# Six context FFN blocks inside the latents' output product, and the next layer's conditioning spread over the FFN

## The chip, the cores and the metric

The kernel runs on one core of a Trainium2 chip. The metric is device time in microseconds (us). The engines are TensorE (PE; its weight loads PEld are listed apart), VectorE (DVE), ScalarE (ACT), GpSimd (POOL) and SyncE (SP), which issues most transfers. Each engine works through its own list in order, so an instruction that waits holds back all that stands behind it on its engine.

## What is computed

Two layers work on 256 latent tokens and 256 context tokens of width 1024. Each layer has three head groups (A, B, C), one output projection, a post-layer-norm, an FFN and a second post-layer-norm; the shifts, scales and gates come from a conditioning product with `w_ada`. The part that matters here is the end of layer 0 and the way into its FFN:

```python
p = jnp.split(_modulate(x, sh1, sc1) @ w_in[li], IN_OFFSETS, axis=-1)     # latents; pc: context
yd, ydc = _diff_attn(p[7], p[8], p[9], pc[7], pc[8], pc[9], ...)          # head group C
mix = jnp.concatenate([ya, yb, yd], axis=-1) @ w_out[li]
x = _post_ln(ALPHA * x + g1 * mix, ln1_g[li], ln1_b[li])
x = _post_ln(ALPHA * x + g2 * ffn(_modulate(x, sh2, sc2)), ln2_g[li], ln2_b[li])
# the same for ctx with yac, ybc, ydc in layer 0
def _swiglu(h, w_gu, w_down):
    g, u = jnp.split(h @ w_gu, 2, axis=-1)
    return (jax.nn.silu(g) * u) @ w_down
```

Context tokens read only context tokens. The FFN of layer 0 has 2816 hidden columns, 22 blocks of 128; layer 1 has eight experts instead.

## The kernel before

**Tiles.** The 512 tokens are four tiles of 128: 0 and 1 are the context, 2 and 3 the latents. Activations are kept transposed in `HI` and `LO` (a rounded part and the rest), 256 columns for each half. Each product is done three times by `mm3`: HI by the weights' rounded part (L273), LO by it (L274), HI by the weights' rest (L276). A weight is loaded to `raw`, rounded by ACT to `whi` (L259), and its rest `wlo` (L260) is made by DVE or POOL. `raw` has 4 buffers, `whi` and `wlo` 3 each.

**How the order comes about.** Generators yield estimated costs; `weave` takes next from the one with the least cost over its weight, `"?name"` waits until some generator has yielded `"+name"`. `PLAN[0]` names the order of the attention tasks: A0 to A3 and C0 to C3 are head groups and tiles, and `/` starts a second stream. What each engine then has in its list is what the rows of order below show.

**The end of layer 0.** `tail0` runs `out_ab` (the output product of groups A and B, PSUM name `op`, 256 columns wide), then `out_c` (that of group C, `op` 512 wide) for each of the pairs (0, 1) and (2, 3). In `attn_C` a tile's scores are `SC`, its weights `P`, transposed to `PT`, its heads `yC`; after an RMS norm (`rstd_of`, tile `nw`, a chain of ten short DVE instructions; L942 applies it) `yC` is transposed (`py`, L952) and split into HI and LO. `CH` names the tiles whose group C is done in two halves. Behind `out_c` comes the post-layer-norm of the tile (`otmp`, L245 statistics, `rstd_of`, L479, L480), then a second layer norm (`layernorm`: statistics, `rstd_of`, `nmr` on DVE, `lnx` on ACT), and `make_hT`, which transposes both tiles of a half on PE (L433, `hT`, 16 of them), modulates them on ACT and leaves the FFN's HI and LO.

**Between.** `ada_group(L1, 0)` follows: sixteen loads of 512 KB of `w_ada` and 64 matmuls (`ada`, L316, two records each in the trace) for layer 1.

**FFN.** `gate_up` makes a block of 128 hidden columns: 2 (gate, up) x 8 (k) x 3 products, 48 matmuls (`gu`), weights of 1 MB in four loads of 256 KB; silu, product, and the split into `ah` and `al`. The first `M0` = 3 blocks are done for the context and then for the latents, 256 columns wide; the other eight of the first half for both, 512 wide. Then the first half of the down product (`dn`), then blocks 11 to 21 and its second half.

Of the kernel before, what the change touches and what calls it, by code (L numbers as in the profile page):

```python
# [12 lines left out]
F = mybir.dt.float32  # L13
# [18 lines left out]
FT = 22  # L32
NE = 8
BIG = 1.0e30
M0 = 3
LOP = 0, 1
KP = 1, 0
XC = 0, 4
LNB, LRB = 3, 7
RO = 2  # L40
CH = (3,), ()
KG = 4
XB, START, MRB, MSB = 1, 1, (5, 1, 5), 4

# [7 lines left out]
TOKT, TRA, ADA = "S", "tp", "S"  # L52
T1, T2, T3, T4, T5, T6, T7, T8, T9 = "y", "tp", "mm", "S", "S", "S", "mm", "tp", "tp"
OPT = 'mm'
HTD = 1
TL0 = CTX, LAT
DNP = 1
DN = ((0, CTX), (1, CTX), (0, LAT), (1, LAT))
# [7 lines left out]

# [48 lines left out]
def kernel(ctx: ExitStack, tc: tile.TileContext, I, out: bass.AP):  # L115
# [21 lines left out]
    def p_(tag, name):  # L137
        return ps.tile([128, 512], F, name=name, tag=tag, bufs=NBUF[tag])
# [79 lines left out]
        return (I["ctx"] if t in CTX else I["x"])[0, (t % 2) * 128:(t % 2 + 1) * 128]  # L218


    def rstd_of(v, n, scale=1.0):


        a = sm.tile([128, 3, 8], F, name="nw", tag="nw", bufs=6)
        ve, y, t = (a[:, i, :n] for i in range(3))
        iv = sm.tile([128, 2, 8], I32, name="nwi", tag="nwi", bufs=6)
# [12 lines left out]
        V.tensor_scalar(y, y, 1.0 / f, None, op0=OP.mult)  # L239
        return y  # L240
# [178 lines left out]

    def layernorm(pool, xs, t):  # L420
        mu, rs = ln_stats(xs[t])
        n = pool.tile([128, D], F, name="lnx", tag="lnx", bufs=LNB if pool is lp else 4)
        nm = sm.tile([128, 1], F, name="nmr", tag="nmr")
        V.scalar_tensor_tensor(nm, mu, -1.0, rs, op0=OP.mult, op1=OP.mult)
        S.activation(n, xs[t], AF.Identity, scale=rs, bias=nm)
        return n
# [76 lines left out]
        return ap.rearrange("p (h d) -> p h d", h=h)  # L503


    def mixers(L, full_ctx, fill, tail):
# [326 lines left out]
        def ssd_finish(t, y):  # L833
            z = zcol(t, 0, 384)
            th = sp.tile([128, 384], F, name="zth", tag="yB", bufs=3)
            S.activation(r4(th, 3), z, AF.Tanh, scale=0.5)
            V.scalar_tensor_tensor(r4(th, 3), r4(th, 3), 1.0, z, op0=OP.add, op1=OP.mult)
            V.scalar_tensor_tensor(y, y, 0.5, th, op0=OP.mult, op1=OP.mult)
            ss = sm.tile([128, 1], F, name="ss", tag="ss")
            S.activation(th, y, AF.Square, accum_out=ss)  # L840
            rs = rstd_of(ss, 1, 1.0 / 384)
            V.scalar_tensor_tensor(y, y, rs, L.snw, op0=OP.mult, op1=OP.mult)
            put_y(t, y, 3, 3)

# [61 lines left out]
        def attn_C(t):  # L906
# [4 lines left out]
            for h in range(4):  # L911
# [25 lines left out]
                if h % 2 and t in CH[li] or h == 3:  # L937
                    a = h - 1 if t in CH[li] else 0
                    n_ = h + 1 - a
                    rs = rstd_of(ss[:, a:h + 1], n_, 1.0 / 64)  # L940
# [101 lines left out]
        weave((1.0, chain(blend(dense_gen(), chain(*fill), nfill, SKIP[li]), tail)),  # L1042
              *((wa[i] if type(wa) is tuple else wa, attention(n)) for i, n in enumerate(streams)), (ws, task("S")))

    def out_consts(L, tiles, pp):

# [80 lines left out]
            post_ln(xs[t], *L.ln1, LN1[t - 2] if L.li else None)  # L1127
            yield t

    def ffn(L, pp, done):  # L1130
        li = L.li
        xs = L.xs
        W = I["ffn_w_gu"][0].rearrange("(k p) (a n) -> p k a n", p=128, a=2)
# [4 lines left out]
        act = {}  # L1138

        def gate_up(f, s):  # L1140
            wk = kpieces(lambda k0: [((slice(None), slice(None), a), W[:, k0:k0 + 4, a, f * 128:(f + 1) * 128])
                                     for a in range(2)], [128, 4, 2, 128])
            o = slice(s.start * 256, s.stop * 256)
            pg = [p_("S", "gu"), p_("mm", "gu")]
            for a in range(2):
                for k0 in range(0, KC, KG):
                    mm3(pg[a][:, o], [(wk(k)[0][:, a], wk(k)[1][:, a], HI[:, s, k], LO[:, s, k], True)
                                      for k in range(k0, k0 + KG)], k0 == 0, k0 + KG == KC)
            sl = L.pp.tile([128, 512], F, name="silu", tag="otmp", bufs=OT)
            S.activation(sl[:, o], pg[0][:, o], AF.Silu)  # L1150
            V.tensor_tensor(sl[:, o], sl[:, o], pg[1][:, o], op=OP.mult)
            if f not in act:
                act[f] = (pp.tile([128, 512], FR, name="ah", tag="ah", bufs=11),
                          pp.tile([128, 512], FR, name="al", tag="al", bufs=11))
            ah, al = act[f]
            S.activation(ah[:, o], sl[:, o], AF.Copy)
            V.tensor_tensor(al[:, o], sl[:, o], ah[:, o].bitcast(F), op=OP.subtract)

        for half in range(2):
            f0 = 11 * half  # L1160
            n0 = 0 if half else M0

            for s in range(2):
                for f in range(f0, f0 + n0):
                    gate_up(f, slice(s, s + 1))
            for f in range(f0 + n0, f0 + 11):
                gate_up(f, slice(0, 2))
            for c, tiles in ((0, (0, 1, 2, 3)), (1, (0, 1, 2, 3))) if half == 0 else DN:
                cs_ = slice(c * 512, (c + 1) * 512)
                tags = ("S", "mm") if len(tiles) == 2 else FDN[c]  # L1170
# [2 lines left out]
                for n in (2, 2, 2, 2, 2, 1):  # L1173
                    src = Wd[f0 * 128:(f0 + n) * 128, cs_].rearrange("(f p) n -> p f n", p=128)
                    wh, wl = split(load_w([(None, src)], [128, n, 512]), [128, n, 512],
                                   G if len(tiles) == 2 and DNP else V)
                    for t in tiles:
                        ts_ = slice(t * 128, (t + 1) * 128)
                        mm3(pd[t], [(*(x[:, ts_] for x in act[f0 + i]), wh[:, i], wl[:, i], False) for i in range(n)],
                            f0 == 11 * half, f0 + n == 11 * half + 11)  # L1180
                    f0 += n
                for t in tiles:
# [539 lines left out]
    def tail0():  # L1722
        yield "?S"
        pp = L0.pp = L0.tp = post.enter_context(tc.tile_pool(name="post0", bufs=1))
        out_consts(L0, range(NT), pp)
        ns = {}
        for tiles in TL0:
            yield from out_ab(L0, tiles, pp)
            for v in out_c(L0, tiles, pp):
                if type(v) is int:  # L1730
                    ns[v] = layernorm(pp, L0.xs, v)
                    if v == 1:
                        if HTD == 1:
                            yield "?att"
                        if HTD < 2:
                            make_hT(pp, L0.mod2, ns, 0)
                    if v == 3:
                        if HTD == 2:
                            make_hT(pp, L0.mod2, ns, 0)
                        make_hT(pp, L0.mod2, ns, 1)  # L1740
# [73 lines left out]
```

## Time and profile before

| | before |
|---|---|
| time, median of 3 runs | 1819.24 us (1816.98 to 1824.41) |
| the profiled execution | 1821.04 us |
| its span in the trace | 1819.2 us |
| PE busy | 1663.7 us, 91% of the span |
| DVE busy | 1154.5 us, 63% |
| ACT busy | 874.4 us, 48% |
| POOL busy | 321.9 us, 18% |
| DMA | 436.09 MB, mean 240 GB/s |

The profiled execution's time is 1.84 us above its span, the part outside the first and the last instruction; its own time is 1.8 us over the median. Busy shares are averages over a program of stages; in the stretch that the change touches (300 to 575 us) every engine has its own limits.

### The profile page before, as it was taken

Reading aid. Unit: us, or ns where it says so; the run is one execution under the profiler, and the core shown is the slowest. Engines: PE = TensorE matmul, PEld = TensorE weight load, DVE = VectorE, ACT = ScalarE, POOL = GpSimd, SP = SyncE. Lnnn points to the kernel's source line nnn. Section 1 sums busy time; section 2 is a strip of 40 time slices with the busy share of each in tenths; the row PEclk is TensorE's granted clock in tenths of the full one; section 3 lists DMA queues with packets and bytes.
Section 4 is the critical chain, followed back from the end, with each engine's and each line's share of the span. In section 5 each row is a group of like instructions: output and inputs, shape, how many; then the busy total and the mean of one; then the engine's idle time right before and its main releaser. Section 6 shows DMA issues by size and latency. Waiting matters only on the chain.

```text
span 1819.2 us, 26372 instructions
## 1 busy us (share of the span) xinstructions
PE 1663.7 (91%) x9454; PEld 1244.2 (68%) x9454; DVE 1154.5 (63%) x2224; ACT 874.4 (48%) x1447; POOL 321.9 (18%) x254
## 2 busy tenths in 40 slices
PE   5898989887999999987999984899999999999995
PEld 2677657674988888876786672487686685784782
DVE  4673668658632343288587756288785586982895
ACT  3433545543622132335444652376673574772770
POOL 1221013334420022474232141000000000000000
PEclk8999998878999999999899996899999999999998
DMA  9327454328633233345676227999999999999995
GB/s 306 86 67 236 127 149 123 107 66 269 188 93 96 89 101 96 110 165 167 209 223 207 65 82 300 395 406 409 408 406 376 399 406 409 406 408 387 408 407 229
DMA packets 248153, 436.09 MB, mean 240 GB/s; under 512 B 15025, under 2 KB 166329, under 8 KB 248017
## 3 DMA queue, kind: packets, MB, share of 16 engines
q1 hardware_dynamic: 246096, 429.55, 66.2%
q0 software_dynamic: 1920, 4.81, 1.0%
q8 instruction: 76, 1.25, 0.3%
q14 instruction: 61, 0.49, 0.1%
HBM read 431.08 MB, written 3.23 MB: 239 GB/s over the span
## 4 chain that ended last, share of the span: by engine, by line
PE 77%; DMA 8%; DVE 7%; issue 2%; ACT 2%; POOL 0%; SPq 0%; ACTq 0%; DVEq 0%; POOLq 0%
PE mg L1369 6%; PE mu L1369 6%; PE mdn L1369 5%; PE gu L273 5%; PE gu L274 5%; PE gu L276 4%; DMA raw<-in_w_ada 4%; PE mu L1358 3%; PE mg L1358 3%; PE mdn L1358 3%; PE tok L276 2%; DMA mraw<-in_exp_w_gu 2%; PE ada L316 2%; PE tok L273 2%; PE SC L919 2%; PE tok L274 2%
## 5 line engine op out<-in xcount | busy, mean ns | idle before, releaser
L1349 DVE TENSOR_TENSOR mwl<-mraw,mwh 128x1024 fp32r<-128x1024 f32 (+1 forms) x350 | 389.4, 1160 | 37.2 <-ACT mwh L1348 20.2
L1348 ACT ACTIVATE mwh<-mraw 128x1024 fp32r<-128x1024 f32 (+1 forms) x350 | 337.8, 1013 | 61.4 <-PE mg L1369 22.9
L260 POOL TENSOR_TENSOR wlo<-raw,whi 128x1024 fp32r<-128x1024 f32 (+2 forms) x93 | 224.1, 2416 | 482.2 <-ACT whi L259 435.1
L259 ACT ACTIVATE whi<-raw 128x1024 fp32r<-128x1024 f32 (+2 forms) x168 | 168.2, 1004 | 237.3 <-PE dn L274 71.9
L260 DVE TENSOR_TENSOR wlo<-raw,whi 128x1024 fp32r<-128x1024 f32 (+2 forms) x75 | 90.5, 1206 | 144.1 <-ACT whi L259 142.8
L273 PE MATMUL gu<-HI,whi 128*128 128x512 f32 (+1 forms) x400 | 144.2, 369 | 2.3 <-ACT whi L259 2.3
L274 PE MATMUL gu<-LO,whi 128*128 128x512 f32 (+1 forms) x400 | 144.9, 369 | 0.0
L273 PE MATMUL tok<-whi,HI 128*128 128x256 f32 (+2 forms) x400 | 108.7, 301 | 5.4 <-ACT xin L550 4.3
L274 PE MATMUL tok<-whi,LO 128*128 128x256 f32 (+2 forms) x400 | 106.4, 295 | 5.2 <-DVE LO L444 5.1
L316 PE MATMUL ada<-raw,cT 128*32 128x256 f32 x768 | 75.5, 430 | 37.8 <-DMA raw<-in_w_ada 35.9
L276 PE MATMUL gu<-HI,wlo 128*128 128x512 f32 (+1 forms) x400 | 98.5, 368 | 0.0
L273 PEld LDWEIGHTS tok<-whi,HI 128*128 128x128 f32 x400 | 79.2, 199 | 14.9 <-issue 5.4
L273 PEld LDWEIGHTS gu<-HI,whi 128*128 128x128 f32 x400 | 75.7, 190 | 15.8 <-ACT whi L259 2.5
L274 PEld LDWEIGHTS tok<-whi,LO 128*128 128x128 f32 x400 | 79.3, 199 | 9.1 <-DVE LO L444 5.8
L274 PEld LDWEIGHTS gu<-LO,whi 128*128 128x128 f32 x400 | 76.1, 191 | 12.8
L276 PEld LDWEIGHTS gu<-HI,wlo 128*128 128x128 f32 x400 | 70.5, 189 | 12.9
L273 PE MATMUL dn<-whi,ah 128*128 128x512 f32 x176 | 70.3, 399 | 5.6 <-ACT whi L259 5.6
L276 PE MATMUL tok<-wlo,HI 128*128 128x256 f32 (+2 forms) x400 | 72.3, 299 | 1.9 <-DVE nw L227 1.9
L1369 PE MATMUL mg<-mwh,Xh 128*128 128x512 f32 x240 | 72.5, 383 | 1.7 <-ACT mwh L1348 1.6
L1369 PE MATMUL mdn<-mwh,mah 128*128 128x512 f32 x220 | 70.1, 400 | 0.9 <-ACT mwh L1348 0.9
L1369 PE MATMUL mg<-mwh,Xl 128*128 128x512 f32 x240 | 70.8, 376 | 0.0
L1369 PE MATMUL mu<-mwh,Xl 128*128 128x512 f32 x240 | 70.7, 376 | 0.0
(361 smaller groups left out, 3496.5 us busy)
## 6 DMA issues: line engine op xcount, KB each, us to landing
mraw<-in_exp_w_gu SPq DMA_DIRECT2D x128, 1024.0 KB, 15.8
mraw<-in_exp_w_down SPq DMA_DIRECT2D x88, 1024.0 KB, 15.6
mraw<-in_exp_w_gu SPq DMA_DIRECT2D x64, 768.0 KB, 13.8
raw<-in_w_ada SPq DMA_DIRECT2D x88, 512.0 KB, 4.8
raw<-in_ffn_w_gu SPq DMA_DIRECT2D x100, 256.0 KB, 3.4
raw<-in_w_in SPq DMA_DIRECT2D x38, 512.0 KB, 5.1
raw<-in_ffn_w_down SPq DMA_DIRECT2D x30, 512.0 KB, 3.7
E<-cscr POOLq DMA_DIRECT2D x12, 384.0 KB, 7.2
```

What stands on the lines that cost most here:

```text
L259: S.activation(hi, raw, AF.Copy)
L260: (eng or V).tensor_tensor(lo, raw, hi.bitcast(F), op=OP.subtract)
L273: T.matmul(o, ah, bh, start=start and i == 0, stop=False)
L274: T.matmul(o, *((ah, bl) if wa else (al, bh)), start=False, stop=False)
L276: T.matmul(o, *((al, bh) if wa else (ah, bl)), start=False, stop=stop and i == n - 1)
L316: T.matmul(pa[32 * j:32 * j + 32, hs], cT[:, k], w[j], start=(k == 0), stop=(k == KC - 1), tile_position=(0, 32 * j), skip_group_check=True)
L919: T.matmul(po[:, :n], qTC(t)[b0:b0 + 32, h // 2], kTC[b0:b0 + 32, h // 2, :n], start=True, stop=True)
L1348: S.activation(wh, raw, AF.Copy)
L1349: V.tensor_tensor(wl, raw, wh.bitcast(F), op=OP.subtract)
L1358: T.matmul(pc[:, :w], xh, wl[:, c * 512:c * 512 + w], start=False, stop=stop)
L1369: T.matmul(pc[:, :w], x, wh[:, c * 512:c * 512 + w], start=start and x is xh, stop=False)
```

## The change

The order of attention: C1 moves from the first stream to the second, so that C0 and C1, the context's tiles, run side by side, and C2 and C3 after them. Tile 3 is no longer done in two halves (`CH`). The context's `make_hT` no longer waits for all attention (`"?att"`). A new generator `ffn_ctx` runs beside the mixers with weight `WF`: when the context's HI and LO are there, it makes six blocks (`M0` = 6) for the context, among the latents' output product, with both PSUM tiles under the tag `mm`, which `op` uses too. The FFN then makes these six for the latents only, 256 wide, and five blocks for both, 512 wide. `ada_group(L1, 0)` is no longer a stretch of its own: one step of it comes behind each `gate_up`. The small `nw` tiles get buffers by kind, the layer norms of layer 0 two `lnx` buffers where they had four, and `ah`, `al` are kept in halves.

```diff
-M0 = 3
+M0 = 6
...
-CH = (3,), ()
+CH = (), ()
...
-HTD = 1
+WF = 2.0
...
-         ("A1", "A0", "A2", "A3", "C0", "C1", "C2", "/", "C3"), 0.7, 0.9, 0.95),
+         ("A1", "A0", "A2", "A3", "C0", "C2", "/", "C1", "C3"), 0.7, 0.9, 0.95),
...
+        a = (lc if kind else sm).tile([128, 3, 8], F, name="nw", tag="nw" + kind, bufs=3)
...
-        n = pool.tile([128, D], F, name="lnx", tag="lnx", bufs=LNB if pool is lp else 4)
+        n = pool.tile([128, D], F, name="lnx", tag="lnx", bufs=LNB if pool is lp else 2)
...
+    def ffn_ctx(L):
+
+        yield "?hTc"
+        for f in range(M0):
+            gate_up(L, f, slice(0, 1), ("mm", "mm"), [act_half(L.pp, 0)])
+            yield 5.7
...
+    def ffn(L, pp, done, side):
...
+            for f in range(f0, f0 + 11):
+                if f < M0:
+                    out = [act_half(pp, 1)]
...
+                gate_up(L, f, slice(int(f < M0), 2), ("S", "mm"), out)
+                next(side, None)
+            for _ in side:
+                pass
...
-                    if v == 1:
-                        if HTD == 1:
-                            yield "?att"
...
+                    if v % 2:
+                        make_hT(pp, L0.mod2, ns, v // 2)
+                        yield 1.7
+                        yield "+hTc"
...
-    mixers(L0, True, [ada_group(L0, 1), ada_group(L0, 2)], tail0())
-    for _ in ada_group(L1, 0):
-        pass
+    mixers(L0, True, [ada_group(L0, 1), ada_group(L0, 2)], tail0(), (WF, ffn_ctx(L0)))
```

How this moves instructions stands at three places; `op`, `ada`, `hT` and `gu` are the PSUM names given above.

**Place 1, PE, up to the context's first `hT`.** Before:

```order
L274 MATMUL op<-whi,LO 128x512
L276 MATMUL op<-wlo,HI 128x512 x2
L316 MATMUL ada<-raw,cT 32x256 x8
L433 MATMUL hT<-cf,lnx 128x128 x2
L273 MATMUL op<-whi,HI 128x512
L274 MATMUL op<-whi,LO 128x512
```

And now:

```order
L865 MATMUL PT<-cf,P 128x128 x4
L932 MATMUL yC<-vC,PT 128x64 x4
L865 MATMUL PT<-cf,P 128x128 x4
L932 MATMUL yC<-vC,PT 128x64 x20
L952 MATMUL py<-cf,yC 128x128 x4
L433 MATMUL hT<-cf,lnx 128x128 x4
L273 MATMUL gu<-HI,whi 128x256 x2
L433 MATMUL hT<-cf,lnx 128x128 x2
L274 MATMUL gu<-LO,whi 128x256 x2
```

Before, the context's first transposes stand among conditioning products and the latents' last output product; now they stand behind the last `py` of all attention, and the first context block is laced with them, ahead of most of the latents' output product.

**Place 2, PE, from the latents' last output product to their `hT`.** Before:

```order
L274 MATMUL op<-whi,LO 128x512
L276 MATMUL op<-wlo,HI 128x512
L316 MATMUL ada<-raw,cT 32x256 x20
L433 MATMUL hT<-cf,lnx 128x128 x4
L316 MATMUL ada<-raw,cT 32x256 x4
L433 MATMUL hT<-cf,lnx 128x128 x2
L316 MATMUL ada<-raw,cT 32x256 x4
L433 MATMUL hT<-cf,lnx 128x128 x4
L316 MATMUL ada<-raw,cT 32x256 x8
L433 MATMUL hT<-cf,lnx 128x128 x4
L273 MATMUL gu<-HI,whi 128x256
L274 MATMUL gu<-LO,whi 128x256
```

And now:

```order
L276 MATMUL op<-wlo,HI 128x512 x2
L433 MATMUL hT<-cf,lnx 128x128 x4
L273 MATMUL gu<-HI,whi 128x256 x2
L316 MATMUL ada<-raw,cT 32x256 x8
L273 MATMUL gu<-HI,whi 128x256 x2
L316 MATMUL ada<-raw,cT 32x256 x4
L433 MATMUL hT<-cf,lnx 128x128 x2
L274 MATMUL gu<-LO,whi 128x256
L433 MATMUL hT<-cf,lnx 128x128 x2
L273 MATMUL gu<-HI,whi 128x256
L274 MATMUL gu<-LO,whi 128x256
```

Before, 36 conditioning matmuls, fourteen of the context's transposes and then the context's first block come behind the last `op`; now the next thing on PE is the latents' own `hT`, and the conditioning stands behind it.

**Place 3, DVE, in the latents' last layer norms.** Before:

```order
L480 SCALAR_TENSOR_TENSOR xr<-xr,nw,bc 128x1024
L245 BN_STATS bst<-xr 128x6 x4
L444 TENSOR_TENSOR LO<-hfull,HI 128x256
L247 BN_AGGR mv<-bst 128x2 x2
L227 TENSOR_SCALAR nw<-mv 128x1 x2
L479 SCALAR_TENSOR_TENSOR xr<-xr,mv,bc 128x1024
L444 TENSOR_TENSOR LO<-hfull,HI 128x256
L228 TENSOR_SCALAR nwi<-nw 128x1 x2
L229 TENSOR_SCALAR nwi<-nwi 128x1 x2
L233 SCALAR_TENSOR_TENSOR nw<-nwi,nw 128x1 x2
L237 SCALAR_TENSOR_TENSOR nw<-nw,nwi 128x1
L444 TENSOR_TENSOR LO<-hfull,HI 128x256
```

And now:

```order
L480 SCALAR_TENSOR_TENSOR xr<-xr,nw,bc 128x1024
L245 BN_STATS bst<-xr 128x6 x4
L247 BN_AGGR mv<-bst 128x2 x2
L227 TENSOR_SCALAR nw<-mv 128x1 x2
L228 TENSOR_SCALAR nwi<-nw 128x1
L479 SCALAR_TENSOR_TENSOR xr<-xr,mv,bc 128x1024
L228 TENSOR_SCALAR nwi<-nw 128x1
L229 TENSOR_SCALAR nwi<-nwi 128x1 x2
L233 SCALAR_TENSOR_TENSOR nw<-nwi,nw 128x1 x2
L237 SCALAR_TENSOR_TENSOR nw<-nw,nwi 128x1 x2
L233 SCALAR_TENSOR_TENSOR nw<-nw 128x1 x2
L237 SCALAR_TENSOR_TENSOR nw<-nw 128x1 x2
```

Before, the context's `LO` stand between the steps of the latents' norms; now these steps follow one another: 58 instructions in a row, from the last `otmp` to the `nmr` that `lnx` waits for, are the latents' norms alone.

## Rows read from the trace of the kernel before

**Rows 1.** Part 4 of the page, the chain that ended last: shares of the span by engine.

```profile
PE 77%; DMA 8%; DVE 7%; issue 2%; ACT 2%; POOL 0%; SPq 0%; ACTq 0%; DVEq 0%; POOLq 0%
```

**Rows 2.** Busy time by engine in stretches of the first layer's end (first row names the columns).

```profile
core 0: us, PE busy (x) PEld busy (x) DVE busy (x) ACT busy (x) POOL busy (x), PEclk, DMA share, GB/s
...
355.00:402.00 47.00, 41.31 (x212) 32.52 (x213) 22.07 (x80) 22.93 (x67) 14.95 (x13) 0.73 0.14 40
...
417.00:448.70 31.70, 21.46 (x172) 9.58 (x171) 27.75 (x96) 11.58 (x22) 11.94 (x11) 0.87 0.92 283
448.70:487.40 38.70, 38.70 (x312) 38.56 (x313) 28.61 (x41) 29.15 (x45) 22.84 (x12) 0.96 0.82 221
487.40:575.00 87.60, 87.60 (x381) 71.36 (x380) 29.72 (x25) 26.00 (x33) 16.90 (x7) 1.00 0.33 98
```

**Rows 3.** Timeline of PE: start us, us, what, [idle before and releaser], and the chain's yC.

```profile
355.02 0.88 PE L952 MATMUL py<-cf,yC 128*128 128x128 f32 x3 [5.50 <-DVE yC L942]
...
382.00 0.88 PE L952 MATMUL py<-cf,yC 128*128 128x128 f32 x3 [3.67 <-DVE yC L942]
...
400.74 0.85 PE yC L932 x8
```

**Rows 4.** Timeline of DVE after 355.

```profile
361.33 0.69 DVE L1118 TENSOR_TENSOR otmp<-op,bc 128x512 f32<-128x512 f32 x1 [0.31 <-PE op L276]
```

**Rows 5.** Groups of PE, 300 to 417: operation, count, busy, mean ns, idle before and releaser.

```profile
L919 PE MATMUL SC<-kTC,YT 32*128 32x512 f32 x30 | 18.6, 774 | 0.0
L932 PE MATMUL yC<-vC,PT 128*128 128x64 f32 x96 | 16.1, 314 | 1.5 <-DVE yC L935 1.5
L865 PE MATMUL PT<-cf,P 128*128 128x128 f32 x48 | 10.9, 369 | 0.5 <-ACT YT L953 0.5
...
L952 PE MATMUL py<-cf,yC 128*128 128x128 f32 x6 | 1.8, 430 | 9.2 <-DVE yC L942 9.2
```

**Rows 6.** Groups of DVE, 355 to 460, columns the same.

```profile
L245 DVE BATCH_NORM_STATS2 bst<-xr 128x6 f32<-128x512 f32 x16 | 10.2, 677 | 0.1
...
L479 DVE SCALAR_TENSOR_TENSOR xr<-xr,mv,bc 128x1024 f32<-128x1024 f32 x4 | 5.6, 1397 | 0.0
```

**Rows 7.** Timeline of DVE and ACT, the latents' last layer norm.

```profile
432.12 0.68 DVE L1118 TENSOR_TENSOR otmp<-op,bc 128x512 f32<-128x512 f32 x1
...
457.68 0.16 DVE L424 SCALAR_TENSOR_TENSOR nmr<-mv,nw 128x1 f32<-128x1 f32 x1
...
457.88 1.25 ACT L425 ACTIVATE lnx<-xr,nmr,nw 128x1024 f32<-128x1024 f32 x1 [0.35 <-DVE nmr L424]
```

**Rows 8.** Groups of PE, 417 to 448.7, and the conditioning's DMA issues there.

```profile
L316 PE MATMUL ada<-raw,cT 128*32 128x256 f32 x128 | 11.7, 470 | 6.5 <-DMA raw<-in_w_ada 4.7 <-DVE rows L324 1.8
L433 PE MATMUL hT<-cf,lnx 128*128 128x128 f32 x16 | 3.8, 351 | 1.1 <-ACT hfull L440 1.0
L273 PE MATMUL op<-whi,HI 128*128 128x512 f32 x8 | 3.3, 430 | 0.4 <-ACT HI L1061 0.4
...
L273 PE MATMUL gu<-HI,whi 128*128 128x256 f32 x1 | 0.4, 388 | 2.3 <-ACT whi L259 2.3
...
raw<-in_w_ada SPq DMA_DIRECT2D x13, 512.0 KB, 6.2
```

**Rows 9.** PE in stretches of the FFN (us, PE busy, PEclk, DMA); a timeline row of PE.

```profile
462.00:478.00 16.00, 16.00 (x139) 1.00 0.70 203
500.00:560.00 60.00, 60.00 (x261) 1.00 0.32 97
...
433.24 1.50 PE L316 MATMUL ada<-raw,cT 128*32 128x256 f32 x24 [1.78 <-DVE rows L324]
```

**Rows 10.** PE in stretches around a wait: us, PE busy (x), PEclk, DMA share, GB/s.

```profile
267.00:270.00 3.00, 0.00 (x0) 0.69 1.00 207
...
272.00:275.00 3.00, 3.00 (x16) 0.50 0.63 168
275.00:278.00 3.00, 3.00 (x28) 1.00 0.48 97
```

More of the change, by code (lines that the diff above doesn't have):

```diff
@@ L218, in x_src, with rstd_of @@
         return (I["ctx"] if t in CTX else I["x"])[0, (t % 2) * 128:(t % 2 + 1) * 128]
-    def rstd_of(v, n, scale=1.0):
-        a = sm.tile([128, 3, 8], F, name="nw", tag="nw", bufs=6)
+    def rstd_of(v, n, scale=1.0, kind=""):
+        a = (lc if kind else sm).tile([128, 3, 8], F, name="nw", tag="nw" + kind, bufs=3)
         ve, y, t = (a[:, i, :n] for i in range(3))
-        iv = sm.tile([128, 2, 8], I32, name="nwi", tag="nwi", bufs=6)
+        iv = (lc if kind else sm).tile([128, 2, 8], I32, name="nwi", tag="nwi" + kind, bufs=3)
         V.tensor_scalar(ve, v, scale, EPS, op0=OP.mult, op1=OP.add)
@@ L503, in r4, with mixers @@
         return ap.rearrange("p (h d) -> p h d", h=h)
-    def mixers(L, full_ctx, fill, tail):
+    def mixers(L, full_ctx, fill, tail, *beside):
         li = L.li
@@ L840, in ssd_finish @@
             S.activation(th, y, AF.Square, accum_out=ss)
-            rs = rstd_of(ss, 1, 1.0 / 384)
+            rs = rstd_of(ss, 1, 1.0 / 384, "S")
             V.scalar_tensor_tensor(y, y, rs, L.snw, op0=OP.mult, op1=OP.mult)
@@ L939, in attn_C @@
                     n_ = h + 1 - a
-                    rs = rstd_of(ss[:, a:h + 1], n_, 1.0 / 64)
+                    rs = rstd_of(ss[:, a:h + 1], n_, 1.0 / 64, "C")
                     yv = y[:, a * 64:(h + 1) * 64]
@@ L1042, in mixers @@
         weave((1.0, chain(blend(dense_gen(), chain(*fill), nfill, SKIP[li]), tail)),
-              *((wa[i] if type(wa) is tuple else wa, attention(n)) for i, n in enumerate(streams)), (ws, task("S")))
+              *((wa[i] if type(wa) is tuple else wa, attention(n)) for i, n in enumerate(streams)), (ws, task("S")),
+              *beside)
     def out_consts(L, tiles, pp):
@@ L1128, in out_c, with gate_up, act_half @@
             yield t
-    def ffn(L, pp, done):
+    def gate_up(L, f, s, tags, out):
+        W = I["ffn_w_gu"][0].rearrange("(k p) (a n) -> p k a n", p=128, a=2)
+        wk = kpieces(lambda k0: [((slice(None), slice(None), a), W[:, k0:k0 + 4, a, f * 128:(f + 1) * 128])
+                                 for a in range(2)], [128, 4, 2, 128])
+        n = 256 * (s.stop - s.start)
+        pg = [p_(tag, "gu") for tag in tags]
+        for a in range(2):
+            for k0 in range(0, KC, KG):
+                mm3(pg[a][:, :n], [(wk(k)[0][:, a], wk(k)[1][:, a], HI[:, s, k], LO[:, s, k], True)
+                                   for k in range(k0, k0 + KG)], k0 == 0, k0 + KG == KC)
+        sl = L.pp.tile([128, 512], F, name="silu", tag="otmp", bufs=OT)[:, :n]
+        S.activation(sl, pg[0][:, :n], AF.Silu)
+        V.tensor_tensor(sl, sl, pg[1][:, :n], op=OP.mult)
+        i, o = s.start, 0
+        for ah, al in out:
+            w = ah.shape[1]
+            S.activation(ah, sl[:, o:o + w], AF.Copy)
+            V.tensor_tensor(al, sl[:, o:o + w], ah.bitcast(F), op=OP.subtract)
+            for c in range(0, w, 256):
+                L.act[f, i] = ah[:, c:c + 256], al[:, c:c + 256]
+                i += 1
+            o += w
+    def act_half(pool, s):
+        return [pool.tile([128, 256], FR, name=n, tag=f"{n}{s}", bufs=M0) for n in ("ah", "al")]
+    def ffn_ctx(L):
[4 more added lines that the diff above has]
+    def ffn(L, pp, done, side):
         li = L.li
         xs = L.xs
-        W = I["ffn_w_gu"][0].rearrange("(k p) (a n) -> p k a n", p=128, a=2)
         Wd = I["ffn_w_down"][0]
@@ L1137, in ffn @@
         b = bc_load(L.pp, I["ln2_b"][li], L.nbc)
[L1138 to L1157, printed above, removed]
         for half in range(2):
             f0 = 11 * half
[L1161 to L1167, printed above, removed]
+            for f in range(f0, f0 + 11):
+                if f < M0:
+                    out = [act_half(pp, 1)]
+                elif f < f0 + M0:
+                    out = [act_half(p, i) for i, p in enumerate((L.pp, pp))]
+                else:
+                    out = [[pp.tile([128, 512], FR, name=n, tag=n, bufs=11 - M0) for n in ("ah", "al")]]
+                gate_up(L, f, slice(int(f < M0), 2), ("S", "mm"), out)
+                next(side, None)
+            for _ in side:
+                pass
             for c, tiles in ((0, (0, 1, 2, 3)), (1, (0, 1, 2, 3))) if half == 0 else DN:
@@ L1177, in ffn @@
                     for t in tiles:
-                        ts_ = slice(t * 128, (t + 1) * 128)
-                        mm3(pd[t], [(*(x[:, ts_] for x in act[f0 + i]), wh[:, i], wl[:, i], False) for i in range(n)],
+                        mm3(pd[t], [(*(x[:, tcol(t)] for x in L.act[f0 + i, t // 2]), wh[:, i], wl[:, i], False)
+                                    for i in range(n)],
                             f0 == 11 * half, f0 + n == 11 * half + 11)
@@ L1685 @@
     L0.li, L1.li = 0, 1
+    L0.act = {}
     L0.nbc, L1.nbc = 4, 5
@@ L1731, in tail0 @@
                     ns[v] = layernorm(pp, L0.xs, v)
-                    if v == 1:
-                        if HTD == 1:
-                            yield "?att"
[L1735 to L1740, printed above, removed]
+                    if v % 2:
+                        make_hT(pp, L0.mod2, ns, v // 2)
+                        yield 1.7
+                        yield "+hTc"
                 else:
                     yield v
-    mixers(L0, True, [ada_group(L0, 1), ada_group(L0, 2)], tail0())
-    for _ in ada_group(L1, 0):
-        pass
+    mixers(L0, True, [ada_group(L0, 1), ada_group(L0, 2)], tail0(), (WF, ffn_ctx(L0)))
     with tc.tile_pool(name="ffn", bufs=1) as fp:
         ffn(L0, fp, lambda tiles: make_hT(L0.pp, L1.mod1, {t: layernorm(L0.pp, L0.xs, t) for t in tiles},
-                                          tiles[0] // 2))
+                                          tiles[0] // 2), ada_group(L1, 0))
     post.close()
```

## The prediction

> **What bounds the kernel now.** I read the chain that ended last, then windows around the place of the change, then the timelines of the engines that PE waits for. Over the whole span PE holds 77% of the chain [rows 1], so work that leaves PE's waits counts and work that only moves on PE does not. The change touches 355 to 575 us, from the contexts' last attention to the start of the down product, 220 us. The windows show four regimes in it [rows 2]. From 355 to 402 the rest of attention runs beside the latents' output product: PE is busy 41.31 of 47 us, at a mean clock of 0.73, and DMA is nearly idle (0.14). PE waits there for a DVE chain: the `py` at 355.02 waits 5.50 us and that at 382.00 3.67 us [rows 3], both for L942, the end of the RMS norm; the last `yC` is at 400.74. From 417 to 448.7 PE is busy only 21.46 of 31.7 us and DMA is at 0.92 and 283 GB/s: the conditioning's weights set the pace, 4.7 us of PE's waits end with them [rows 8]. From there on PE is never idle, 38.70 and 87.60 us busy of as many.
>
> **The pace of PE.** In the blocks 256 wide 139 matmuls took 16 us, 0.115 us each; in those 512 wide 261 took 60 us, 0.230 each [rows 9]. So 512 columns cost the same whether done in one piece or two: making six blocks instead of three in halves costs nothing on PE, only three more blocks of weights loaded twice. A conditioning record takes 1.50/24 = 0.0625 us [rows 9]; 128 of them are 8 us. PE's work is the same before and after; only its waits move. The question is what they are, stage by stage, and I add up the new order from 355 to `dn`.
>
> **a) Until the context's first hT.** Now C0 and C1 end together. Their `py` stands some ten PE instructions and some eight DVE instructions later in its list than the first `py` before, so I put it 3 us later, at 358. Then two things run side by side. On PE stand 101 instructions up to the first `hT`: 24 `op` of 512 and 18 of 256 (7.6 us by the pace), and by the groups [rows 5] 24 `PT` (0.227 each, 5.5), 32 `yC` (0.168, 5.4), four `py` (0.3, 1.2) and two `SC` (0.62, 1.2): 21 us. On DVE stand 117 instructions up to the last L942, which the last `py` needs: both context post-layer-norms, most of both layer norms, and the latents' heads and RMS chains, all in one list. In the two windows DVE took 22.07/80 = 0.276 and 27.75/96 = 0.289 us for an instruction [rows 2], so 33 us. It can't start at 358: the first `otmp` came 6.3 us after `py` (355.02 to 361.33) [rows 3, 4], for the way goes over ACT and the output product. With 5 us in which DVE itself waits (PE's wait for each was 4 to 5 us) the first `hT` comes at 358 + 6 + 33 + 5 = 402. Bounds: 392 without the two smaller terms, 410 if the waits are twice as long. Since the order places `hT` behind all attention, the six context blocks do not run beside attention at all; they run beside the latents' output product, and both want PE.
>
> **b) The context's hT and first block**, laced k by k: 16 transposes at 0.351 us, 5.6 [rows 8], and 48 matmuls, 5.5: 11 us (9 if the transposes hide, 13 with ACT's waits): 413.
>
> **c) Five context blocks amid 126 `op`** of 256: 240 + 126 matmuls at 0.115 = 42 us. Blocks and `op` share the two `mm` tiles and the three split buffers, so each change from one to the other waits for the silu or a split. No row shows this; the nearest are the first `gu`, 2.3 us for its `whi`, and `op`, 0.4 us for HI [rows 8]. Six changes lie between 2.4 and 13.8 us; I take 8: 463.
>
> **d) The latents' 24 `op` of 512**: 5.5 us: 468.5. Before, nearly the same stood in 417 to 448.7.
>
> **e) The latents' norms.** Here the cover goes. Before, the way from the last `otmp` (432.12) to the end of `lnx` (457.88 + 1.25) took 27 us [rows 7] and cost nothing, for behind the last `op` PE had conditioning, the context's `hT` and the context's blocks (place 2 of the order). Now PE's next instruction is the latents' `hT`. DVE has 58 instructions to do, each behind the one before: at 0.276 to 0.289 they take 16 to 17 us; since large ones (seven L245 of 0.68, two L479 of 1.40 [rows 6], two L480 as wide) are more frequent among them than in those windows, I take 18. Plus `lnx`, 1.25: **19.5 us** of idle PE, from 16 to 24 (the 27 us of before had the context's `LO` and splits of weights between them). It ends at 488.
>
> **f) The latents' six blocks**: 288 matmuls 33.1 us, 96 conditioning records 6, `hT` 4 (half of its 5.6 + 1.1 hides). After its wait at 267 PE ran at 0.50 for some 5 us before it was back at 1.00 [rows 10], that is at 1.2 of 2.4 GHz: 2.5 us lost. The loads are 6 x 1.05 MB of blocks and 12 x 0.52 MB of conditioning, 12.6 MB, 44.5 us at 283 GB/s [rows 2]; part of them comes during e). Together 47 us (43 to 53): 535.
>
> **g) Five blocks of 512** and 32 records: 55.2 + 2 = 57 (56 to 60): 592.
>
> 592 against 575: **17 us more**. The profiled execution's own time, 1821.04 us, becomes 1838; it lies 1.8 us above the median, so on that basis 1836. What is saved is the stretch of the conditioning with its 10 us of idle PE; what is lost is cover, in a) 20 us in which PE had the latents' output product to do, in e) 19.5. Costed at nothing: the new buffers by kind (`nw`), two `lnx` where four were (both of a pair live at once, the next pair later), halves of `ah`, and layer 1, whose order hardly moves.
>
> **What the pages say.** The Trainium skill, Perfetto Trace Analysis, section Optimization Strategy, says that where the most contended engine changes over time, interleaving those regimes may improve performance. That speaks for this change: conditioning, bound by DMA, goes beside blocks bound by PE. By it alone the idle 10.2 us of 417 to 448.7 would be won and nothing lost, 1809; that is rival A's time, and it shares A's chance. Against it stands that the same page's regime at 355 to 402, bound by DVE, is not interleaved here but laid bare.
>
> **Rivals.** **A, faster.** DVE does not set a): the two latents' heads and the context's norms fit into the gaps, and PE's own 21 us do, so the first `hT` comes at 358 + 21 = 379 less the 3 us that I added, 376. That is 26 us earlier: 566, 9 less than before, 1810. It decides from there down: `hT` at 376 is the point. For it speaks that DVE was busy only 22.07 of 47 us there [rows 2]; against it that `py` waited for DVE both times. **B, no change**: a) at 392, the waits of c) 3, e) 17, f) 44: 392 + 10 + 45 + 5.5 + 17 + 44 + 57 = 570.5, 4.5 less, 1815. The same holds up to 584, that is, if all of a) is as supposed but e) is half covered. **C, slower still**: the latents' blocks are bound by their loads, 12.6 MB at the 221 GB/s of 448.7 to 487.4 [rows 2], 57 us, and each change in c) costs 2.3: 10 + 6 more, 608, 1852. For it speaks the DMA share of 0.82 there, against it that a third of the loads can come in the wait e).
>
> **Chances.** My forecast (9 to 27 us more, 1828 to 1846) 0.42; B 0.25; C 0.20; A 0.13. Half a per cent, 9 us, is about what a measurement of this kernel tells from no change. Faster by more is A, 0.13; within it B, 0.25; slower the forecast and C, 0.62. The range from A's upper part to C: 1809 to 1853 leaves out about half of A and a little of C.
>
> **What would show it.** In the profile after: the first context `hT` near 402, with DVE busy all the way up to it and PE idle some 15 us; `gu` of 256 laced with `op` from 413; after the last `op` of 512 one wait of PE of 16 to 24 us, ended by `lnx`, then half clock; conditioning without a stretch of its own; `dn` first at 592. Wrong, if `hT` comes before 380, if that wait is under 10 us, or if the latents' blocks wait for `raw` more than 5 us.

## The result, and the profile after

| | before | changed |
|---|---|---|
| median | 1818.34 us (1816.98 to 1824.41, 4 runs) | 1840.91 us (1836.67 to 1850.34, 4 runs) |
| span of the profiled execution | 1819.2 us | 1834.9 us |
| `py` of the context to the first `dn` | 220.3 us | 237.4 us |

The ratio is 1.0125, 95% interval 1.0094 to 1.0156: slower, 22.6 us in the medians and 15.7 us in the two profiled spans. The stretch that the change touches, from the first `py` after 350 us to the down product, became 17.1 us longer (355.02 to 575.3 us before, 357.22 to 594.57 us now). 234 us were predicted for it, 592 less 358; it took 237.4. (With the old order of attention that first `py` ends one context tile, with the new one two, so this stretch compares best among kernels of one order.)

First the windows of the changed kernel, cut at the steps a) to g) of the prediction (c and d in one); the first row names the columns:

```profile
core 0: us, PE busy (x) PEld busy (x) DVE busy (x) ACT busy (x) POOL busy (x), PEclk, DMA share, GB/s
357.22:399.47 42.25, 28.89 (x151) 24.47 (x151) 33.79 (x118) 18.40 (x48) 11.62 (x9) 0.70 0.18 45
399.47:411.90 12.43, 11.46 (x66) 9.32 (x65) 4.10 (x9) 11.08 (x23) 3.63 (x5) 0.79 0.07 22
411.90:465.50 53.60, 50.64 (x391) 47.96 (x390) 27.93 (x31) 23.32 (x31) 35.94 (x20) 1.00 0.57 168
465.50:488.10 22.60, 0.72 (x3) 0.29 (x2) 20.37 (x60) 3.54 (x3) 7.66 (x4) 0.59 0.43 137
488.10:536.20 48.10, 47.06 (x401) 39.51 (x401) 15.84 (x23) 22.05 (x38) 12.69 (x9) 0.94 0.70 208
536.20:594.60 58.40, 58.40 (x278) 45.92 (x276) 19.85 (x19) 17.90 (x22) 12.02 (x5) 1.00 0.53 159
```

| step | predicted, us | measured, us |
|---|---|---|
| a) `py` to the context's `hT` | 44 | 42.3 |
| b) `hT` and first block | 11 | 12.4 |
| c), d) five blocks amid the latents' product | 55.5 | 53.6 |
| e) latents' norms | 19.5 | 22.6 |
| f) latents' six blocks | 47 | 48.1 |
| g) five blocks of 512 | 57 | 58.4 |

Two rows carry the loss. In e) PE is busy 0.72 of 22.6 us and DVE 20.37. In a) PE is busy 28.89 of 42.25 us, at a mean clock of 0.70. In c), d) and g) PE is busy almost all of the time, at 1.00. The waits of PE from 405 us to the down product, by what ended them (total, times, longest):

```profile
PE hT L433 <- ACT lnx L425: 21.9, 2, 17.5
PE gu L273 <- DVE otmp L1091: 1.5, 2, 0.8
PE gu L273 <- ACT whi L259: 1.0, 3, 0.5
```

The 21.9 us for `lnx` are e); before, PE waited nowhere for it. The waits that sharing PSUM and split buffers was supposed to bring, 8 us in c), are the rows below it, 1.5 and 1.0 us, and a few smaller ones. The timeline of PE at the two places (start, us, what, idle before and releaser):

```profile
357.22 1.11 PE L952 MATMUL py<-cf,yC 128*128 128x128 f32 x4
...
379.09 1.97 PE L932 MATMUL yC<-vC,PT 128*128 128x64 f32 x8 [0.65 <-DVE yC L935]
381.72 1.97 PE L932 MATMUL yC<-vC,PT 128*128 128x64 f32 x8 [0.66 <-DVE yC L935]
384.36 1.97 PE L932 MATMUL yC<-vC,PT 128*128 128x64 f32 x8 [0.67 <-DVE yC L935]
...
399.02 0.66 PE L952 MATMUL py<-cf,yC 128*128 128x128 f32 x2 [3.97 <-DVE lcst L402]
399.47 1.37 PE L433 MATMUL hT<-cf,lnx 128*128 128x128 f32 x4
...
483.03 0.69 PE L433 MATMUL hT<-cf,lnx 128*128 128x128 f32 x2 [17.50 <-ACT lnx L425]
488.13 0.69 PE L433 MATMUL hT<-cf,lnx 128*128 128x128 f32 x2 [4.41 <-ACT lnx L425]
```

The `py` of 357.22 answers to that of 355.02 in [rows 3]. Between it and the context's `hT` at 399.47 stand groups of eight `yC`, 1.97 us each, with 0.66 us of waiting for DVE between them. The mean clock there (us, PE busy, PEclk, DMA share, GB/s):

```profile
376.00:399.00 23.00, 11.57 (x46) 0.53 0.17 43
```

Half of 23 us is idle, and what PE does, it does at 0.53, close to the lower level of 1.2 GHz; no single wait in it is longer than 4 us.

### The profile page after: what moved, and what is told of

The parts are those of the page before. It is cut to its first block, busy times and chain, and to the rows that moved or that the text cites. A ratio compares the mean times of both kernels' runs of the same rounds, so it can differ in the third digit from the quotient of the medians.

```text
span 1834.9 us, 26718 instructions
## 1 busy us (share of the span) xinstructions
PE 1667.4 (91%) x9598; PEld 1251.1 (68%) x9598; DVE 1158.7 (63%) x2225; ACT 880.8 (48%) x1463; POOL 335.1 (18%) x256
## 4 chain that ended last, share of the span: by engine, by line
PE 60%; DVE 7%; DMA 4%; ACT 2%; issue 2%; POOL 1%; SPq 0%; ACTq 0%; DVEq 0%; POOLq 0%
PE mg L1387 6%; PE mu L1387 6%; PE mdn L1387 5%; PE gu L273 4%; PE gu L274 4%; PE gu L276 4%; PE mg L1376 3%; PE mu L1376 3%; PE mdn L1376 3%; PE mg L1542 2%; PE dn L273 2%; PE dn L276 2%; PE dn L274 2%; DMA mraw<-in_exp_w_gu 2%; PE mdn L1576 2%
## 5 line engine op out<-in xcount | busy, mean ns | idle before, releaser
L260 POOL TENSOR_TENSOR wlo<-raw,whi 128x1024 fp32r<-128x1024 f32 (+2 forms) x96 | 234.8, 2452 | 491.7 <-ACT whi L259 436.4
L259 ACT ACTIVATE whi<-raw 128x1024 fp32r<-128x1024 f32 (+2 forms) x174 | 174.3, 1006 | 260.5 <-PE dn L274 74.6
L273 PE MATMUL gu<-HI,whi 128*128 128x512 f32 (+1 forms) x448 | 149.5, 352 | 2.9 <-DVE otmp L1091 1.5
L274 PE MATMUL gu<-LO,whi 128*128 128x512 f32 (+1 forms) x448 | 149.2, 349 | 0.4 <-POOL LO L444 0.3
L273 PEld LDWEIGHTS gu<-HI,whi 128*128 128x128 f32 x448 | 84.4, 191 | 19.0 <-ACT whi L259 2.4
L274 PEld LDWEIGHTS gu<-LO,whi 128*128 128x128 f32 x448 | 84.5, 190 | 12.7 <-POOL LO L444 0.9
```

The costliest lines, as they stand in the source:

```text
L259: S.activation(hi, raw, AF.Copy)
L260: (eng or V).tensor_tensor(lo, raw, hi.bitcast(F), op=OP.subtract)
L273: T.matmul(o, ah, bh, start=start and i == 0, stop=False)
L274: T.matmul(o, *((ah, bl) if wa else (al, bh)), start=False, stop=False)
```

## The experiments

Each is compared with the kernel before on the same chip. "py to dn" is the stretch of the table above, in the one profiled execution.

| run | median, us | ratio, 95% interval | py to dn, us |
|---|---|---|---|
| three blocks kept back | 1840.94 | 1.0103 (1.0063 to 1.0143) | 234.3 |
| conditioning in one stretch | 1839.77 | 1.0102 (1.0068 to 1.0136) | 231.3 |
| before, conditioning spread | 1831.33 | 1.0060 (1.0038 to 1.0081) | 229.5 |
| old order of attention | 1849.09 | 1.0155 (1.0116 to 1.0194) | 250.0 |
| no post-layer-norm | 1829.11 | 1.0050 (1.0027 to 1.0073) | 225.0 |
| all six blocks kept back | 1819.11 | 1.0002 (0.9980 to 1.0025) | 217.6 |
| the same again | 1821.80 | 1.0007 (0.9982 to 1.0033) | 216.9 |
| before, six blocks | 1819.15 | 0.9990 (0.9968 to 1.0012) | 217.1 |
| before, new order | 1817.31 | 0.9975 (0.9946 to 1.0004) | 209.7 |
| five blocks kept back | 1842.84 | 1.0108 (1.0065 to 1.0152) | 230.1 |
| three kept back, rest made on DVE | 1839.86 | 1.0104 (1.0069 to 1.0139) | 231.1 |
| before, new order and six blocks | 1816.11 | 0.9981 (0.9956 to 1.0006) | 209.9 |

**Three blocks kept back.** They are emitted between the latents' second layer norm and their `hT`:

```diff
-        for f in range(M0):
+        for f in range(M0 - 3):
             gate_up(L, f, slice(0, 1), ("mm", "mm"), [act_half(L.pp, 0)])
...
+                    if v == 3:
+                        for f in range(M0 - 3, M0):
+                            gate_up(L0, f, slice(0, 1), ("S", "mm"), [act_half(pp, 0)])
```

> The changed kernel, with three of the six context blocks kept back until behind the latents' last output product, where PE waits 17.5 and 4.4 us for the latents' norms. Theory (cover): the loss is that wait and the bare attention before the context's hT, nothing else. Three blocks are 144 matmuls of 0.115 us, 16.6 us; they fill the wait but for some 5 us, less 2 us that their silu and splits add to the norms on DVE and ACT: 15 us faster than the changed kernel, about 1826. Rival (spread): the conditioning and the context blocks' second loads make the latents' blocks wait; then moving the blocks changes nothing, 1841. Rival (order): the attention's new order is the loss; 1841 as well.

Measured: no gain in the median, 3.1 us in py to dn. The three blocks do stand in the wait, and yet PE waits there, in other places (total, times, longest):

```profile
PE hT L433 <- ACT lnx L425: 11.0, 2, 6.5
PE gu L276 <- DVE wlo L260: 4.0, 1, 4.0
```

From the end of the last output product (452.29) to the latents' second `hT` (485.75) it now takes 33.5 us, not 22.6. So the cover made the thing that it covers longer. DVE's timeline shows how; these are steps of the norm chain:

```profile
460.67 2.33 DVE L237 SCALAR_TENSOR_TENSOR nw<-nw,nwi 128x1 f32<-128x1 f32 x1
...
464.34 3.52 DVE L480 SCALAR_TENSOR_TENSOR xr<-xr,nw,bc 128x1024 f32<-128x1024 f32 x1
...
475.68 2.44 DVE L233 SCALAR_TENSOR_TENSOR nw<-nw 128x1 f32<-128x1 f32 x2
```

An L237 took 0.16 us elsewhere in this chain, an L480 1.28. POOL's timeline at these times:

```profile
460.57 2.42 POOL L260 TENSOR_TENSOR wlo<-raw,whi 128x1024 fp32r<-128x1024 f32 x1
464.36 2.41 POOL L260 TENSOR_TENSOR wlo<-raw,whi 128x1024 fp32r<-128x1024 f32 x1 [1.37 <-ACT whi L259]
475.74 2.36 POOL L260 TENSOR_TENSOR wlo<-raw,whi 128x1024 fp32r<-128x1024 f32 x1 [8.97 <-DVE nw L237]
```

Each late DVE instruction stands beside a weight split on POOL. The two on one column are done when the split is; the L480 is done 1.1 us after it, about its own 1.28. The Trainium skill, SBUF — State Buffer, section Terms, says that DVE and GpSimd share one pair of ports, held by one of them for the whole instruction while the other blocks; these rows agree.

**That claim tried: the rest of these three blocks' weights on DVE alone.**

```diff
-    def gate_up(L, f, s, tags, out):
+    def gate_up(L, f, s, tags, out, kp=KP):
...
+                            gate_up(L0, f, slice(0, 1), ("S", "mm"), [act_half(pp, 0)], (0, 0))
```

> The kernel with three blocks kept back, but the weights' rest of these three made on DVE alone, not on POOL and DVE in turn. In that kernel the way from the last output product to the latents' second hT took 33.5 us, against 22.6 in the changed kernel, and four times a DVE instruction ended together with a POOL split that ran beside it, some 2.1 us late. Theory (POOL's split holds DVE): DVE does three to four splits more at 1.22 us and loses the four waits of 2.1: 30 us, between 28 and 32. Rival (DVE is merely fuller): 33.5 plus the splits, 37 to 39 us.

From the end of the last output product, at 448.93, to the second `hT` of the latents (the second row, PE) it takes 30.3 us, within the theory's 28 to 32: DVE does more, and is done earlier.

```profile
474.12 0.69 PE L433 MATMUL hT<-cf,lnx 128*128 128x128 f32 x2 [9.62 <-ACT lnx L425]
479.23 0.69 PE L433 MATMUL hT<-cf,lnx 128*128 128x128 f32 x2 [4.41 <-ACT lnx L425]
```

3 us of 33.5 came back, but not all of these meetings are gone. POOL still splits weights for the latents' blocks behind, and two DVE instructions beside it are late (first the two on DVE, then the two splits):

```profile
459.94 3.33 DVE L480 SCALAR_TENSOR_TENSOR xr<-xr,nw,bc 128x1024 f32<-128x1024 f32 x1
...
467.80 2.85 DVE L479 SCALAR_TENSOR_TENSOR xr<-xr,mv,bc 128x1024 f32<-128x1024 f32 x1
...
459.76 2.43 POOL L260 TENSOR_TENSOR wlo<-raw,whi 128x1024 fp32r<-128x1024 f32 x1 [6.80 <-ACT whi L259]
...
467.23 2.34 POOL L260 TENSOR_TENSOR wlo<-raw,whi 128x1024 fp32r<-128x1024 f32 x1 [5.04 <-DVE wlo L260]
```

Over the 1.28 us that each takes elsewhere that is 3.6 us of the 7.7 by which 30.3 still exceeds 22.6. The rest is put down to the blocks' own work on DVE (splits, silu's product, `al`) between the steps of the norms, which no run separates.

**The conditioning in one stretch again, under the change.**

```diff
+    for _ in ada_group(L1, 0):
+        pass
     with tc.tile_pool(name="ffn", bufs=1) as fp:
...
-                                          tiles[0] // 2), ada_group(L1, 0))
+                                          tiles[0] // 2), iter(()))
```

> The changed kernel, with the next layer's conditioning again as one stretch ahead of the FFN; 104 of its 128 records then stand between the latents' last output product and their hT. Theory (cover): the wait of 22 us stays but holds about 6 us of conditioning, which no longer stand in the FFN: 6 to 8 us faster than the changed kernel, 1834; the 8.4 MB of loads need 30 us at 283 GB/s, so 3 us may be lost again. Rival (spread): conditioning beside the blocks is the loss, and it goes: 17 us or more faster, 1823 or less. Rival (order): no more than the 6 us.

6.1 us less in py to dn, as the cover theory said; the median is only 1.1 us lower, with runs between 1828.74 and 1852.71, which can't tell 6 us. The 21.9 us of waiting for `lnx` became

```profile
PE ada L316 <- DMA raw<-in_w_ada: 8.3, 8, 2.2
PE hT L433 <- ACT lnx L425: 4.1, 1, 4.1
```

and the wait for the conditioning's loads: the stretch covers the norms, and is slow for its loads, as it was before [rows 8].

**The conditioning spread, in the kernel before.**

```diff
-    for _ in ada_group(L1, 0):
-        pass
...
                     gate_up(f, slice(s, s + 1))
+                    next(side, None)
...
                 gate_up(f, slice(0, 2))
+                next(side, None)
```

> The kernel before, with this alone of the change: the conditioning's steps behind the FFN's blocks in place of a stretch of their own. Theory (cover): the stretch had 10 us of idle PE that are won; the context's hT and first blocks follow the last output product directly and the latents' norms hide behind the context's three blocks (16.6 us) all but some 5 us: 5 us faster than before, 1813, between 1808 and 1819. Rival (spread): the conditioning's loads beside those of the blocks are what costs the changed kernel its time: 10 us or more slower than before, 1828 and up.

The theory's number was wrong here, by its sign: 1.0060, and 9.2 us more in py to dn. PE's waits from 400 us to the down product:

```profile
PE hT L433 <- ACT lnx L425: 8.8, 2, 7.1
PE op L276 <- DVE wlo L260: 3.2, 1, 3.2
PE ada L316 <- DMA raw<-in_w_ada: 3.2, 5, 0.9
PE gu L273 <- ACT HI L438: 1.7, 2, 1.2
PE gu L274 <- DVE LO L444: 1.2, 2, 0.9
PE gu L274 <- POOL LO L444: 1.2, 1, 1.2
```

The stretch of conditioning had covered not only the latents' norms but also the context's: the context's `hT` stands ahead of the last output products in PE's list, and without conditioning before it PE waits 7.1 us for its `lnx`; then the first block waits for HI and LO piece by piece, 4.1 us in three rows. The time is the rival's (1828 and up), its reason is not: PE waits 3.2 us for the conditioning's loads beside the blocks, less than the 4.7 us of the stretch [rows 8].

**The old order of attention, under the change.**

```diff
-         ("A1", "A0", "A2", "A3", "C0", "C2", "/", "C1", "C3"), 0.7, 0.9, 0.95),
+         ("A1", "A0", "A2", "A3", "C0", "C1", "C2", "/", "C3"), 0.7, 0.9, 0.95),
...
-CH = (), ()
+CH = (3,), ()
```

> The changed kernel, with the attention's old order (C0, C1, C2 in one stream, C3 in the other, tile 3's group C in two halves). Theory (cover): the context's hT still stands behind the last py, which waits for the DVE list, and the wait for the latents' norms is untouched: within 6 us of the changed kernel, 1841, the first context hT between 395 and 408. Rival (order): the new order lays DVE's list bare, and the old one gives back the 18 us between the attention's end on PE and the hT: 1823.

Slower than the changed kernel by 8 us in the median, so the new order is not the loss. The first context `hT` came at 404.0, within the span of the first theory, and the down product began at 602.5, not 594.6; the time itself lies outside the 6 us that this theory allowed. What makes these 8 us stays open.

**No post-layer-norm in layer 0.** Its statistics, its rstd chain and its affine part are left out for all tiles, so the values that follow are not the reference's:

```diff
-            post_ln(xs[t], *L.ln1, LN1[t - 2] if L.li else None)
+            if L.li:
+                post_ln(xs[t], *L.ln1, LN1[t - 2] if L.li else None)
```

> The changed kernel without the post-layer-norm behind the output product of layer 0, for all four tiles (its statistics, rstd chain, L479 and L480 are left out; the second layer norm stays). About 6 us of DVE work per tile go. Theory (DVE list sets both waits): the context's first hT comes 10 to 12 us earlier after the contexts' py than in the changed kernel (42 us there, 30 to 32 here), and the 22 us from the last output product to the latents' second hT become 9 to 12. Rival (attention's own chain through PE, ACT and DVE sets the first): the hT no more than 3 us earlier, and only the second wait falls.

The timeline of PE at the two places:

```profile
356.49 1.11 PE L952 MATMUL py<-cf,yC 128*128 128x128 f32 x4
...
397.03 1.36 PE L433 MATMUL hT<-cf,lnx 128*128 128x128 f32 x4
...
472.18 0.69 PE L433 MATMUL hT<-cf,lnx 128*128 128x128 f32 x2 [9.64 <-ACT lnx L425]
473.31 0.69 PE L433 MATMUL hT<-cf,lnx 128*128 128x128 f32 x2 [0.45 <-ACT lnx L425]
```

In e) the theory held: from the last output product's end (462.54) to the latents' second `hT` it takes 10.8 us in place of 22.6. In a) it fell. DVE's work between 357 and 402 us became less, here in the changed kernel and then without the norm (us, DVE busy and count, PEclk, DMA share, GB/s):

```profile
357.00:402.00 45.00, 35.02 (x122) 0.69 0.17 43
```

```profile
357.00:402.00 45.00, 25.47 (x94) 0.70 0.16 43
```

9.6 us less, and the `hT` came 40.5 us after `py`, 1.7 us earlier than the 42.25 of the changed kernel. So the rival was right about a): each head's eight `yC` go over ACT to DVE (L935), whose end lets the next head start, and PE, with nothing else to do, runs them at half clock.

**All six blocks kept back**, the edit of the first experiment with 6 for 3.

> The changed kernel with all six context blocks kept back until behind the latents' output product; the conditioning stays spread. The output product then stands beside attention again. Theory (cover): the bare attention is covered as before, and the latents' norms by 33 us of blocks, so that only what the spread conditioning cost alone (10 us over the kernel before) is left: 1829, between 1822 and 1836. Rival (weaving costs nothing, the spread conditioning and six blocks' doubled loads are the loss): as the changed kernel, 1841.

Against the kernel before all of the loss is gone, though the conditioning stays spread and six blocks are done twice: 10 us better than was expected. Heads of the last attention and the clock over them:

```profile
378.22 1.00 PE L932 MATMUL yC<-vC,PT 128*128 128x64 f32 x8
...
393.04 1.00 PE L932 MATMUL yC<-vC,PT 128*128 128x64 f32 x8
```

```profile
376.00:399.00 23.00, 19.82 (x164) 1.00 0.46 138
```

Eight `yC` take 1.00 us, since the latents' output product runs between the heads (the 23 us that were half idle hold 164 PE records, not 46). This kernel was run once more:

> The kernel with all six context blocks kept back, once more and in more rounds: with the conditioning spread, the six blocks as cover of the latents' norms. Theory: the same as the kernel before within 0.3%: 1816 to 1824. Rival (the earlier runs were fast by chance, the spread conditioning costs its 10 us here too): 1829.

1821.8 us, 1.0007: as the kernel before.

**One block left in the weave**, the same edit with 5.

> The changed kernel with five of the six context blocks kept back behind the latents' output product; one block stays woven into it. Theory (a queue's head): one block is enough to hold back the output product's 126 matmuls, for it takes its split and PSUM buffers ahead of them and waits for the context's hT; so attention stays bare: the yC of the last heads take 1.97 us for eight at half clock, the first hT comes 41 to 43 us after the contexts' py, and from py to the down product it takes 224 to 230 us, against 217.6 with all six kept back and 237.4 in the changed kernel. Rival (each woven block costs its share): 221, the eight at 1.0 us.

The time is that of the changed kernel, and heads, first `hT` and clock are, too:

```profile
382.00 1.97 PE L932 MATMUL yC<-vC,PT 128*128 128x64 f32 x8 [0.66 <-DVE yC L935]
...
391.12 1.97 PE L932 MATMUL yC<-vC,PT 128*128 128x64 f32 x8 [0.66 <-DVE yC L935]
...
399.76 1.37 PE L433 MATMUL hT<-cf,lnx 128*128 128x128 f32 x4
```

```profile
376.00:399.00 23.00, 11.35 (x46) 0.54 0.14 29
```

The `hT` comes 42.5 us after `py`; py to dn is 230.1 us, 0.1 us above the theory's span. A single block is enough to lay attention bare. In py to dn it costs 12.5 us over all six kept back; the medians lie 23.7 us apart. The rest lies outside of this stretch: after the down product's start the two profiled executions take 1255.6 and 1238.2 us, and others of these kernels anything between. Why that part differs is not settled.

**The parts that were not slower**, in the kernel before: `M0 = 6` alone, the order and `CH` alone, and both.

> The kernel before, with this alone: six blocks done for the context and then for the latents instead of three. PE's work is the same, 3.1 MB more weights are loaded. Theory: the loads have room (DMA share 0.33 from 487 us on), so 0 to 4 us: 1821 to 1825. Rival (doubled loads cost): the six blocks of the latents and of the context need 12 x 1.05 MB at 221 GB/s, 57 us against 66 us of PE, so no; but if weights' splits on ACT, DVE and POOL (twelve blocks more often than PE needs at 512) are the limit, 10 us or more: 1831.

> The kernel before, with this alone: the new order of attention (C1 in the second stream) and tile 3's group C undivided. Theory (order is not the cause): within 5 us of the kernel before, 1816 to 1826. Rival (order): 10 us or more slower, 1831.

> The kernel before with the two parts that were not slower by themselves: the new order of attention, and six blocks in halves. Theory: both are neutral to small gains (py to down product 209.7 and 217.1 us against 220.3): 1815, between 1808 and 1820. Rival (both only moved the start of the window): 1820.

All three are within the interval of no change (0.9990, 0.9975, 0.9981). py to dn is 10 us shorter with the new order, 209.7 and 209.9, but the `py` itself comes later there (360.65 and 357.31, not 355.02), since it now ends two tiles and not one. So six blocks done twice cost nothing that these runs show, and the best of these kernels gains at most half a per cent.

The last of them is also the closest comparison for the kernel with all six kept back, since order and `M0` agree and the last run of each has 12 executions. With conditioning spread and six blocks kept back it is slower, 1821.80 to 1816.11 us in medians of overlapping runs (1815.28 to 1829.92 and 1807.89 to 1828.17), and 216.9 to 209.9 us in py to dn. So what is left of the change does not look free even with cover; whether the spreading, the blocks' place or the new buffers cost this was not separated.

## Why the prediction was right

**The sum.** 17 us more were forecast and 17.1 came in the stretch; the medians moved by 22.6. Each step lies within 3.5 us of its measure. That is partly luck, for step a) was right in its size and wrong in its reason. It is also partly the marker, for the first `py` itself moved. From the last `py` of group B ahead of it (308.96 before, 303.68 now) to `dn` it took 266.3 us before and takes 290.9 now, 24.6 more. Between the two markers 46.1 us became 53.5; the prediction put 3 us there for these 7.5. Against the kernel before with the new order and six blocks (209.9), py to dn is 27.5 us longer.

**Step a), the step that failed.** The prediction put "On DVE stand 117 instructions up to the last L942" as the bound, 33 us of DVE work. Leaving out 9.6 us of DVE work took 1.7 us off. What holds the context's `hT` is attention's own chain, head by head, at half clock on a PE that has nothing else. PE's side was too small as well, 21 us where PE was busy 28.89: a `yC` instruction leaves two records in the trace, so the 32 counted are 64 records and took 12.9 us (40 of them at half clock), not 5.4. And in the last RMS chain DVE waits 1.46 us for a load of the next layer's constants (L398, `in_attn_sink`) that stands in its list there; in the kernel before it waits for nothing there. And why PE has nothing else is not what the prediction said either ("Since the order places `hT` behind all attention"): the context's `hT` stands there with all six blocks kept back as well (414.87, right behind the last `py` at 414.41), and the loss is gone. What counts is that the 126 matmuls of the latents' output product stand behind the first context block. One woven block does that, 230.1 us against 217.6; with six woven, and so no cover for e), it is 237.4. That the block's split and PSUM buffers, taken ahead of the output product's, are what forces this place fits all orders here, but was not tried apart from the place itself.

**Step e)** was right, as a mechanism and nearly in size: 22.6 against 19.5 us. Without the post-norm it falls to 10.8. 2.1 of the missing 3 us are one L237 that took 2.26 us in place of 0.16, beside a split on POOL (DVE and POOL of the changed kernel):

```profile
470.91 2.26 DVE L237 SCALAR_TENSOR_TENSOR nw<-nw,nwi 128x1 f32<-128x1 f32 x1
...
473.46 0.16 DVE L237 SCALAR_TENSOR_TENSOR nw<-nw 128x1 f32<-128x1 f32 x1
...
470.82 2.33 POOL L260 TENSOR_TENSOR wlo<-raw,whi 128x1024 fp32r<-128x1024 f32 x1
```

**Step c)** was over-sized: of the 8 us of waits for shared buffers PE's idle time in c) and d) leaves 3.0. **Step f)**: the conditioning's loads beside the blocks did not bind; no wait for `raw` appears among PE's waits after 405 us. The terms listed for f) add up to 45.6 us, not 47; it took 48.1.

**What is saved** was read wrongly: "the stretch of the conditioning with its 10 us of idle PE". The stretch's idle time was cover for two norms; the kernel before loses 9.2 us in py to dn when the conditioning is taken out of it. With enough other work in that place (six blocks kept back) the same spreading costs nothing against the kernel before, and gains nothing; against the kernel before with the new order and six blocks, what is left of the change is 7.0 us longer in py to dn.

**Rival A** (PE's own 21 us set a), **rival B** (the first `hT` at 392) and **rival C** (loads bind f) are refuted by the windows: a) took 42 us and ended at 399.5, and f) took 48.1. A's first half, that DVE does not set a), came true. The Trainium skill, Perfetto Trace Analysis, section Optimization Strategy, says that interleaving regimes may improve performance. Here it did not: blocks bound by PE were put beside an output product bound by PE, and the stretch bound by attention's chain lost the product that had filled it.

## What to carry to other kernels

When work is woven in earlier, look at what stands behind it in the same engine's list and the same buffer pools: a piece that waits for a late input can push back all that was ready, and here one piece laid attention as bare as six did (the `hT` 42.5 and 42.3 us after `py`). Idle time in a stretch is not yet a gain; ask which waits of other work it covers, and what the replacement needs on the engine that makes those waits, since a cover that puts its splits on the norms' engine makes the norms longer. And take a right total with care: leaving out the suspected work (9.6 us of it) showed in one run that the engine named was not the bound.

## What the hardware showed

A vector instruction on one column (L237, 0.16 us) took 2.26 and 2.33 us when a POOL split of 128x1024 ran beside it. And PE's clock fell to a mean of 0.53 over 23 us in which no wait was longer than 4 us and PE was busy half of the time; the same eight matmuls took 1.97 us there and 1.00 us with the output product between them.
